# A two-layer hybrid decoder step: FFN up projections as seven products of halves, the gated product kept in DRAM, the down projection in three groups

## The chip, the cores and the metric

The kernel runs on one core of one Trainium2 chip. The core has a matrix engine (TensorE, PE in the profile, with its weight loads as PEld), a vector engine (VectorE, DVE), an activation engine (ScalarE, ACT), GpSimd (POOL), and a queue engine (SyncE, SP) from which this kernel issues all its DMAs. SBUF is the on-chip memory of 128 partitions; PSUM is where TensorE writes, and this kernel has five PSUM banks for its main products and three for side work. The metric is the device time of one execution in microseconds.

## The reference

One inference step of a two-layer decoder for 1024 prompt positions and 8 x 8 sample positions, 1088 columns in all, model width 1024. Layer 0 mixes with a convolution module and a retention in parallel, layer 1 with a gated linear recurrence. Each mixer is followed by the same gated convolution FFN, and this is where the change lies:

```python
def _conv_ffn(h, buf, w_up, conv_w, conv_b, w_down):
    z = h @ w_up
    zc, new_buf = _causal_dwconv(z, buf, conv_w, conv_b)
    g, u = jnp.split(zc, 2, axis=-1)
    return (jax.nn.gelu(g) * u) @ w_down, new_buf
```

Here `h` is the RMS-normalised residual (1088 x 1024), `w_up` is 1024 x 5632 (2816 gate and 2816 value columns), the convolution runs over positions with width 3, and `w_down` is 2816 x 1024. The result is added to the residual. The last two rows of `z` of each sequence are an output too. All arithmetic is float32.

## The kernel before

Everything is kept feature-major: 128 features on the partitions, positions as columns. `X` (8 feature tiles of 1088 columns) is the residual. A matrix product in float32 is made of three TensorE matmuls: each operand is split into a rounded high part and a low part that is the rest, and `mm3` (line 157) adds high x high, high x low and low x high in one PSUM bank. `HH` and `HL` hold the two parts of the normalised residual. Every `matmul` call comes with its own weight load. Columns are cut into blocks `TT` of 384, 384 and 320.

Weights come as 188 tiles of 128 x 1024 in a fixed order. `load_to` (line 111) fetches one into a raw buffer, lets ACT write the high part (line 118) and DVE the low part (line 119), and `get_w` (line 123) stays a stated number of tiles ahead.

The program text gives an order of emission. The framework that builds the kernel puts the instructions on each engine in that priority, and takes a later one first if the earlier one isn't ready by its own reckoning; each engine then works its queue strictly in order. Work that rides along (norms, retention, gates) is written as generators in the list `side`; after every sixth main matmul one step of the first generator is emitted (`mm`, `tick`, lines 151 and 135). `flush` emits what is left.

`rmsnorm` (line 183) does one column block: squares on ACT and sums on DVE, a transpose and a reduction, the root, a transpose back, then for each of eight feature tiles a scaling on DVE (line 224) and a split (lines 179 and 180). The output projections (`out_proj`, line 242, and the end of `even_mixer`) do their last feature tiles block by block, so that the norm of one block rides along under the next block's matmuls.

`ffn` (line 266) walks over 22 pairs, each a gate tile and a value tile of 128 features. `pair` (line 276) makes the two up products, 8 k tiles x 3 matmuls for each of the three column blocks, and ACT copies them from PSUM to `Z` rows. `act` (line 302) does the convolution with three DVE instructions a tile (lines 307 to 309), the GELU on ACT (line 314), the gated product on DVE (line 316), and its split into `A` (lines 319 to 323). POOL copies the edges of `Z` (lines 284, 311 and 312). `down` (line 327) follows two pairs behind: it multiplies the `A` of two pairs with their down weights and adds each 128 x 384 result to `X` (`add_x`, line 176). The last four pairs go together, block by block, with the next norm behind each block.

Of the kernel before, what the change touches and what calls it, by code (L numbers as in the profile page):

```python
# [26 lines left out]
# column offsets in the packed parameter tile  # L27
# [12 lines left out]
# columns of the shape-only constants of the retention  # L40
# [40 lines left out]
def hybrid_step(ctx: ExitStack, tc: tile.TileContext, I, O):  # L81
# [5 lines left out]
    wpool = ctx.enter_context(tc.tile_pool(name="wpool", bufs=5))  # L87
    rawp = ctx.enter_context(tc.tile_pool(name="rawp", bufs=2))
    tmpp = ctx.enter_context(tc.tile_pool(name="tmpp", bufs=5))
# [10 lines left out]
    HH = big.tile([P, KD, NT], F32R, name="HH")  # L100
    HL = big.tile([P, KD, NT], F32R, name="HL")
# [5 lines left out]
    # ---------------------------------------------------------------- weights  # L107
    state = {"loaded": 0, "next": 0}
    wtiles = {}

    def load_to(n):
        while state["loaded"] < min(n, len(ORDER)):
            i = state["loaded"]
            raw = rawp.tile([P, 1024], F32, tag="raw", name="raw")
            nc.sync.dma_start(raw, I["w"][i])
            ws = wpool.tile([P, 2, KD, P], F32R, tag="ws", name="ws")
            whi = ws[:, 0].rearrange("p k f -> p (k f)")
            nc.scalar.activation(whi, raw, AF.Copy)  # L118
            nc.vector.tensor_tensor(ws[:, 1].rearrange("p k f -> p (k f)"), raw, whi.bitcast(F32), ALU.subtract)  # L119
            wtiles[i] = ws  # L120
            state["loaded"] += 1
# [8 lines left out]
    # Work that rides along: generators whose steps are emitted between the  # L130
    # matmuls of the main stream, one step to about a microsecond of them.
# [9 lines left out]

    def flush(gen=None):
        """Emits what is left of the generators up to gen, or of all."""
# [7 lines left out]
    def mm(out, lhsT, rhs, start, stop):  # L151
        nc.tensor.matmul(out, lhsT, rhs, start=start, stop=stop)  # L152
        count[0] += 1
        if count[0] % TICK == 0:
            tick()

    def mm3(out, w_hi, w_lo, x_hi, x_lo, start, stop):
        mm(out, w_hi, x_hi, start, False)
        mm(out, w_hi, x_lo, False, False)
        mm(out, w_lo, x_hi, False, stop)  # L160

    def mm_group(ws, t):
        """Weight tiles over one column block, the contraction outermost."""
        t0, n = TT[t]
        pss = [mmp.tile([P, 512], F32, tag="mm", name="mm") for _ in ws]
        for k in range(KD):
            for w, ps in zip(ws, pss):
                mm3(ps[:, :n], w[:, 0, k], w[:, 1, k], HH[:, k, t0:t0 + n], HL[:, k, t0:t0 + n], k == 0, k == KD - 1)
        return pss

# [11 lines left out]
    # ------------------------------------------------- 1/sqrt of column sums  # L182
    def rmsnorm(t, g, final=False, spill_after=False):
        """RMSNorm of one column block of X into HH and HL, or into the output (a generator)."""
        t0, n = TT[t]
        acc = tmpp.tile([P, 512], F32, tag="tmp", name="acc")
        for m in range(KD):
            if m == 0:
                nc.scalar.activation(acc[:, :n], X[:, m, t0:t0 + n], AF.Square)
            else:  # L190
                sq = tmpp.tile([P, 512], F32, tag="tmp", name="sq")
# [24 lines left out]
        for m in range(KD):  # L216
# [6 lines left out]
            hn = tmpp.tile([P, 512], F32, tag="tmp", name="hn")  # L223
# [5 lines left out]
    # residual to DRAM and back, one column block at a time  # L229
# [11 lines left out]
    # ------------------------------------------------------ output projection  # L241
    def out_proj(key, norm_g):
        NE = 3
        for m in range(NE):
            w = get_w((key, m))
            for t in range(3):
                add_x(m, t, mm_tile(w, t))
        ws = [get_w((key, m), ahead=KD - 1 - m) for m in range(NE, KD)]
        for t in range(3):
# [757 lines left out]
```

## Time and profile before

| | |
|---|---|
| median of 3 runs | 2389.2 us (2389.01 to 2390.93) |
| profiled execution: span | 2388.6 us |
| profiled execution: its own time | not listed apart; the median lies 0.6 us above the span |
| PE busy | 2362.4 us, 99%, 14368 matmuls |
| PEld busy | 2332.5 us, 98% |
| DVE busy | 1463.3 us, 61% |
| ACT busy | 811.9 us, 34% |
| POOL busy | 154.7 us, 6% |
| mean granted TensorE clock | 0.996 |
| DMA | 133.28 MB, mean 56 GB/s |

The page gives the busy time of each engine, the chain of work that ended last (each step followed back to what released it), and the costliest groups of instructions: line, engine, operation, output and input tiles, count, then busy time and mean duration of one, then the idle time of the engine ahead of them and what ended it. A window row has the busy time and instruction count of each engine in a stretch, the granted clock as a share of full, the share of the DMA engines and GB/s. A timeline row has the start in us, the duration, the engine, the line and the instruction. Matmul records overlap, so their busy time isn't the sum of their durations.

### The profile page before, as it was taken

To read this page: it belongs to the slowest core of one execution; us is meant where nothing else is said; L and a number is where in the kernel's file an instruction comes from. 1 tells how busy PE (TensorE), PEld (TensorE's weight loads), DVE (VectorE), ACT (ScalarE), POOL (GpSimd) and SP (SyncE) were. 2 spreads that over 40 slices of the span, in tenths; PEclk is the share of its full clock that TensorE was granted. 3 is DMA by queue.
4 is the path that set the end of the run, shared out by engine and by line. 5 is a ranking of instruction groups with operands and counts; after the bars stand their busy time and mean duration, and the time that the engine had idled before them with its cause. 6 is when DMAs were issued, how large, how long until landed. Compare 5 with 4: busy or idle time off the path is not lost.

```text
span 2388.6 us, 34372 instructions
## 1 busy us (share of the span) xinstructions
PE 2362.4 (99%) x14368; PEld 2332.5 (98%) x14368; DVE 1463.3 (61%) x2209; ACT 811.9 (34%) x1500; POOL 154.7 (6%) x409
## 2 busy tenths in 40 slices
PE   9999999999999999999999999999999999999998
PEld 8999999999999999999999999999999999999997
DVE  6899965575554455555467757476455555455546
ACT  6334437342222222222235667243222222222222
POOL 0000000010000000000000211001000000000000
PEclk9999999999999999999999999999999999999999
DMA  5212114111111111111113111411111111111102
GB/s 181 67 46 64 55 37 115 39 62 44 45 36 54 45 45 45 45 36 54 45 60 131 36 36 36 119 45 54 45 45 45 45 36 54 45 45 45 45 29 80
DMA packets 64509, 133.28 MB, mean 56 GB/s; under 512 B 24097, under 2 KB 37281, under 8 KB 64225
## 3 DMA queue, kind: packets, MB, share of 16 engines
q1 hardware_dynamic: 64352, 131.08, 17.4%
q8 instruction: 113, 1.85, 0.3%
q14 instruction: 44, 0.35, 0.1%
HBM read 118.28 MB, written 12.78 MB: 55 GB/s over the span
## 4 chain that ended last, share of the span: by engine, by line
PE 93%; DVE 3%; ACT 2%; DMA 1%; issue 1%; DVEq 0%; SPq 0%; ACTq 0%
PE mm L152 89%; DVE acc L193 1%; PE ax L852 0%; PE ax L545 0%; PE ax L536 0%; DMA X<-in_x 0%; DVE ws L119 0%; PE ax L527 0%; PE ax L507 0%; PE ax L495 0%; PE ax L759 0%; DVE X L774 0%; PE ax L479 0%; PE ax L529 0%; PE ax L760 0%
## 5 line engine op out<-in xcount | busy, mean ns | idle before, releaser
L152 PE MATMUL mm<-HH,ws 128*128 128x384 f32 (+1 forms) x6912 | 1715.5, 328 | 0.6 <-ACT HH L854 0.5
L152 PEld LDWEIGHTS mm<-HH,ws 128*128 128x128 f32 x6912 | 1223.3, 188 | 8.9 <-issue 6.8
L152 PE MATMUL mm<-HL,ws 128*128 128x384 f32 (+1 forms) x3456 | 1129.2, 327 | 4.1 <-DVE HL L180 4.1
L152 PEld LDWEIGHTS mm<-HL,ws 128*128 128x128 f32 x3456 | 650.0, 188 | 5.1 <-DVE HL L180 4.7
L152 PE MATMUL mm<-A,ws 128*128 128x384 f32 (+1 forms) x3168 | 528.0, 328 | 0.4 <-ACT A L319 0.4
L152 PEld LDWEIGHTS mm<-A,ws 128*128 128x128 f32 x3168 | 522.5, 188 | 1.3 <-ACT A L319 1.0
L119 DVE TENSOR_TENSOR ws<-raw,ws 128x1024 fp32r<-128x1024 f32 x188 | 228.0, 1222 | 306.7 <-ACT ws L118 306.5
L176 DVE TENSOR_TENSOR X<-X,mm 128x384 f32<-128x384 f32 (+1 forms) x540 | 277.2, 530 | 157.2 <-PE mm L152 148.4
L118 ACT ACTIVATE ws<-raw 128x1024 fp32r<-128x1024 f32 x188 | 197.1, 1059 | 395.9 <-PE mm L152 390.6
L307 DVE TENSOR_SCALAR Y<-Z,par 128x1104 f32<-128x1104 f32 x88 | 74.8, 852 | 273.7 <-ACT Z L299 273.7
L295 ACT ACTIVATE Z<-mm 128x384 f32<-128x384 f32 x176 | 86.7, 493 | 360.1 <-PE mm L152 360.0
L413 DVE SCALAR_TENSOR_TENSOR X<-U,par,X 128x1024 f32<-128x1024 f32 x120 | 151.7, 1280 | 0.0
L311 POOL COPY fst<-Z 128x2 f32<-128x2 f32 x88 | 52.2, 593 | 1181.6 <-ACT Z L298 1181.6
L319 ACT ACTIVATE A<-Y 128x1024 fp32r<-128x1024 f32 x44 | 46.7, 1062 | 222.0 <-DVE Y L316 222.0
L308 DVE SCALAR_TENSOR_TENSOR Y<-Z,par,Y 128x1104 f32<-128x1104 f32 x88 | 120.2, 1367 | 2.3
L309 DVE SCALAR_TENSOR_TENSOR Y<-Z,par,Y 128x1104 f32<-128x1104 f32 x88 | 120.1, 1366 | 1.5
L298 ACT ACTIVATE Z<-mm 128x256 f32<-128x256 f32 x88 | 33.0, 375 | 126.9 <-PE mm L152 126.9
L322 DVE TENSOR_TENSOR A<-Y,A 128x1024 fp32r<-128x1024 f32 x44 | 53.8, 1223 | 29.3 <-ACT A L319 29.3
L314 ACT ACTIVATE Y<-Y 128x1104 f32<-128x1104 f32 x44 | 49.6, 1128 | 54.7 <-DVE Y L309 54.7
L192 ACT ACTIVATE sq<-X 128x384 f32<-128x384 f32 (+1 forms) x84 | 39.8, 502 | 77.4 <-DVE X L176 69.8
L316 DVE TENSOR_TENSOR Y<-Y 128x1104 f32<-128x1104 f32 x44 | 57.4, 1305 | 0.8
L193 DVE TENSOR_TENSOR acc<-acc,sq 128x384 f32<-128x384 f32 (+1 forms) x84 | 44.9, 534 | 16.3 <-ACT sq L192 12.1
(193 smaller groups left out, 1229.9 us busy)
## 6 DMA issues: line engine op xcount, KB each, us to landing
raw<-in_w SPq DMA_DIRECT2D x188, 512.0 KB, 3.5
X<-in_xt SPq DMA_DIRECT2D x8, 512.0 KB, 7.9
X<-in_x SPq DMA_DIRECT2D x4, 768.0 KB, 5.3
spill<-X SPq DMA_DIRECT2D x2, 1536.0 KB, 5.8
X<-spill SPq DMA_DIRECT2D x2, 1536.0 KB, 10.3
out_y<-X SPq DMA_DIRECT2D x4, 768.0 KB, 3.4
S<-in_st_ret SPq DMA_DIRECT2D x4, 512.0 KB, 3.5
out_s_ret<-S SPq DMA_DIRECT2D x4, 512.0 KB, 2.6
```

The source lines that it names most:

```text
L118: nc.scalar.activation(whi, raw, AF.Copy)
L119: nc.vector.tensor_tensor(ws[:, 1].rearrange("p k f -> p (k f)"), raw, whi.bitcast(F32), ALU.subtract)
L152: nc.tensor.matmul(out, lhsT, rhs, start=start, stop=stop)
L176: nc.vector.tensor_tensor(X[:, m, t0:t0 + n], X[:, m, t0:t0 + n], ps[:, :n], ALU.add)
L193: nc.vector.tensor_tensor(acc[:, :n], acc[:, :n], sq[:, :n], ALU.add)
L295: nc.scalar.activation(z[:, 2 + t0:2 + t0 + n], ps[:, :n], AF.Copy)
L307: nc.vector.tensor_scalar(y, z[:, 2:NE], pc(fw, 2 * 44 + f), pc(fb, f), ALU.mult, ALU.add)
L308: nc.vector.scalar_tensor_tensor(y, z[:, 1:NE - 1], pc(fw, 44 + f), y, ALU.mult, ALU.add)
L309: nc.vector.scalar_tensor_tensor(y, z[:, 0:NE - 2], pc(fw, f), y, ALU.mult, ALU.add)
L316: nc.vector.tensor_tensor(Y[0], Y[0], Y[1], ALU.mult)
L322: nc.vector.tensor_tensor(a[:, 1, :NP], y[:, :NP], a[:, 0, :NP].bitcast(F32), ALU.subtract)
L413: nc.vector.scalar_tensor_tensor(cv, U[i][:, j:j + NP], wj, cv, ALU.mult, ALU.add)
```

## The change

The up projection of one pair is a product of a 1024 x 256 weight (two k halves x gate and value tile) with 1024 x 1088 activations (two k halves x two column halves of 544). After, it is made by a scheme of seven products of halves (Winograd's form of Strassen's algorithm) in place of the eight: each product has 4 k tiles and 272 columns, twice, for the two blocks `SB` of each half. Sums of operands are made before the products and sums of results after:

- `norm_halves` takes the place of `rmsnorm` ahead of an FFN. It works on blocks `TB` (208, 208 and 128 columns of each column half), stores the residual to DRAM (`spill`), scales `X` in place, and writes seven split operands: four into `HB` (the old `HH` and `HL`), three into a new tile `HX`.
- `Pair` loads the two raw weight tiles of a pair and makes seven split weight operands of 128 x 512, with four combinations on DVE, the high parts on ACT and the low parts on POOL. The next pair's are made while a pair's products run, two steps in its first half block and the rest in its second.
- `block` runs the seven products of one half block in four PSUM banks (three of them are accumulated into again after they were read) and adds up the results into `Z`.
- `X` is free during the up products and holds `Z`, `Y` and the other rows of the FFN.
- `act` starts the convolution on ACT in place of DVE (Identity with scale and bias); the gated product isn't split, but stored to DRAM (`yd`).
- The down projection comes after all 22 pairs, in three groups of 8, 6 and 8 feature tiles. `fetch` loads a stored product and splits it, into `HB` for the first and third group and `A2` for the second. The first group's result is added to the stored residual, which makes `X` again; the others are added to `X`.
- The last four feature tiles of an output projection run in the blocks `TB` (`proj_tail`), weight tiles are split in two halves (`wpool` of 10 half tiles in place of 5 whole), and the general temporaries are 4 of 544 columns in place of 5 of 512.

```diff
+NH = NT // 2
+TB = [(0, 208), (208, 208), (416, 128)]
+SB = [(0, 272), (272, 272)]
+GROUPS = (8, 6, 8)
...
     for p in range(NFF):
         o += [("up%d" % l, p), ("up%d" % l, NFF + p)]
-        if p % 2 == 0 and 2 <= p <= NFF - 4:
-            o += [("dn%d" % l, p - 2), ("dn%d" % l, p - 1)]
-    o += [("dn%d" % l, q) for q in range(NFF - 4, NFF)]
+    o += [("dn%d" % l, (g, m)) for g in range(len(GROUPS)) for m in range(KD)]
...
+    class Pair:
+        def steps(self):
+            r1, r2 = self.raws
+            a11, a12, a21, a22 = r1[:, :512], r1[:, 512:], r2[:, :512], r2[:, 512:]
+            def put(src):
+                w, hi, lo = split_w(src)
+                nc.gpsimd.tensor_tensor(lo, src, hi.bitcast(F32), ALU.subtract)
+                self.w.append(w)
+            v = nc.vector
+            s3 = self.pool.tile([P, 512], F32, tag="s3", name="s3", bufs=1)
+            v.tensor_tensor(s3, a11, a21, ALU.subtract)
+            put(a11)
+            yield
+            v.tensor_tensor(a21, a21, a22, ALU.add)
+            put(s3)
+            yield
+            put(a21)
+            yield
+            v.tensor_tensor(a11, a21, a11, ALU.subtract)
+            put(a11)
+            yield
+            put(a12)
+            yield
+            v.tensor_tensor(a12, a12, a11, ALU.subtract)
+            put(a22)
+            yield
+            put(a12)
...
+    def norm_halves(b, g, spill, HX):
+        o, n = TB[b]
+        N = 2 * n
+        nc.sync.dma_start(spill, halves(X, o, n))
...
+        for kk in (0, 2):
+            for k in (kk, kk + 1, kk + 4, kk + 5):
+                xm = halves(X[:, k], o, n)
+                nc.vector.scalar_tensor_tensor(xm, xm, pc(g, k), rb, ALU.mult, ALU.mult)
...
+            def put(src, k, c):
+                hi, lo = (HB[(slice(None), e) + part(k, c)] if c < 2 else HX[:, e, c - 2, kk:kk + 2, o:o + n]
+                          for e in (0, 1))
+                nc.scalar.activation(hi, src, AF.Copy)
+                nc.vector.tensor_tensor(lo, src, hi.bitcast(F32), ALU.subtract)
...
+            put(b11, kk, 0)
+            t3 = diff(b22, b12)
+            put(t3, None, 3)
+            t1 = diff(b12, b11)
+            put(t1, kk, 1)
+            t2 = diff(b22, t1)
+            put(t2, None, 2)
+            put(b21, kk + 4, 0)
+            t4 = diff(b21, t2)
+            put(t4, None, 4)
+            put(b22, kk + 4, 1)
+            yield
...
+    def proj_tail(m0, ws, ffn):
+        ffn.start()
+        for b in range(3):
+            o, n = TB[b]
+            for m, w in enumerate(ws):
+                ps = mm_halves(w, HACTS, b)
+                xm = halves(X[:, m0 + m], o, n)
+                nc.vector.tensor_tensor(xm, xm, ps, ALU.add)
+                if b == 2:
+                    ffn.first.make(2)
+            side.append(ffn.norm(b))
...
+            MOVE = (0, 5, 1, 4, 2, 6, 3)
+            def product(w, i, sb, ps, first):
+                o, n = SB[sb]
+                for k in range(4):
+                    mm3(ps[:, :n], w[:, 0, k], w[:, 1, k], moving(MOVE[i], 0, k, o, n), moving(MOVE[i], 1, k, o, n),
+                        first and k == 0, k == 3, more=not first)
...
+                p1 = bank()
+                product(W.w[0], 0, sb, p1, True)
+                nc.scalar.activation(u2[:, :n], p1[:, :n], AF.Copy)
+                after(0)
+                p7 = bank()
+                product(W.w[1], 1, sb, p7, True)
+                after(1)
+                p5 = bank()
+                product(W.w[2], 2, sb, p5, True)
+                after(2)
+                p6 = bank()
+                product(W.w[3], 3, sb, p6, True)
+                v.tensor_tensor(u2[:, :n], u2[:, :n], p6[:, :n], ALU.add)
+                v.tensor_tensor(u3[:, :n], u2[:, :n], p7[:, :n], ALU.add)
+                high(z2, u3, p5)
+                after(3)
+                product(W.w[4], 4, sb, p1, False)
+                nc.scalar.activation(low(z1), p1[:, :n], AF.Copy)
+                after(4)
+                product(W.w[5], 5, sb, p7, False)
+                v.tensor_tensor(low(z2), u2[:, :n], p7[:, :n], ALU.add)
+                after(5)
+                product(W.w[6], 6, sb, p5, False)
+                high(z1, u2, p5)
+                after(6)
...
+                    nc.scalar.activation(y, z[:, 2:NE], AF.Identity, bias=pc(fb, f), scale=pc(fw, 2 * 44 + f))
+                    v.scalar_tensor_tensor(y, z[:, 1:NE - 1], pc(fw, 44 + f), y, ALU.mult, ALU.add)
+                    v.scalar_tensor_tensor(y, z[:, 0:NE - 2], pc(fw, f), y, ALU.mult, ALU.add)
...
+                nc.sync.dma_start(self.yd[p], YG)
...
+            def fetch(f, sb, hi, lo):
+                o, n = SB[sb]
+                t = tmpp.tile([P, 544], F32, tag="tmp", name="yl")
+                tv = t.rearrange("p (h c) -> p h c", h=2)
+                nc.sync.dma_start(tv, halves(self.yd[f], o, n))
+                nc.scalar.activation(halves(hi, o, n), tv, AF.Copy)
+                v.tensor_tensor(halves(lo, o, n), tv, halves(hi, o, n).bitcast(F32), ALU.subtract)
+            W = self.first
+            W.make(8)
+            flush_all_but_last()
+            for p in range(NFF):
+                if p:
+                    prepare(p)
+                nxt = self.pair(p + 1) if p + 1 < NFF else None
+                def after_a(i):
+                    if nxt and i in (3, 6):
+                        nxt.make()
+                def after_b(i):
+                    if nxt:
+                        nxt.make()
+                    else:
+                        fetch(i, 0, *HACTS[i])
+                block(p, W, 0, after_a)
+                if p:
+                    act(p - 1)
+                flush()
+                if not p:
+                    prepare(p)
+                block(p, W, 1, after_b)
+                if nxt:
+                    nxt.make(8)
+                W = nxt
+            fetch(7, 0, *HACTS[7])
+            load_to(state["next"] + 3)
+            for q in range(8):
+                fetch(q, 1, *HACTS[q])
+            act(NFF - 1)
...
+                def first_block(w, m, b):
+                    o, n = TB[b]
+                    t = tmpp.tile([P, 544], F32, tag="tmp", name="xr")
+                    tv = t[:, :2 * n].rearrange("p (h c) -> p h c", h=2)
+                    nc.sync.dma_start(tv, self.spill[b][:, m])
+                    ps = mm_halves(w, HACTS, b)
+                    v.tensor_tensor(halves(X[:, m], o, n), tv, ps, ALU.add)
...
+                for m in range(4):
+                    w = get_w((key, (2, m)), ahead=3)
+                    for t in range(3):
+                        add_x(m, t, down(w, HACTS, t))
+                ws = [get_w((key, (2, m)), ahead=KD - 1 - m) for m in range(4, KD)]
+                for t in range(3):
+                    for m in range(4, KD):
+                        add_x(m, t, down(ws[m - 4], HACTS, t))
+                    side.append(rmsnorm(t, norm_next, final, spill_after=not final))
```

More of the change, by code (lines that the diff above doesn't have):

```diff
@@ L140, in tick, with flush_all_but_last @@
                 side.popleft()
+    def flush_all_but_last():
+        while len(side) > 1:
+            for _ in side.popleft():
+                pass
     def flush(gen=None):
@@ L149, in flush, with mm @@
                 break
-    def mm(out, lhsT, rhs, start, stop):
-        nc.tensor.matmul(out, lhsT, rhs, start=start, stop=stop)
+    def mm(out, lhsT, rhs, start, stop, more=False):
+        nc.tensor.matmul(out, lhsT, rhs, start=start, stop=stop, skip_group_check=more)
         count[0] += 1
@@ L155, in mm, with mm3 @@
             tick()
[L157 to L160, printed above, removed]
+    def mm3(out, w_hi, w_lo, x_hi, x_lo, start, stop, more=False):
+        mm(out, w_hi, x_hi, start, False, more)
+        mm(out, w_hi, x_lo, False, False, more)
+        mm(out, w_lo, x_hi, False, stop, more)
     def mm_group(ws, t):
@@ L185, in rmsnorm @@
         t0, n = TT[t]
[L186 removed]
+        acc = tmpp.tile([P, 544], F32, tag="tmp", name="acc")
         for m in range(KD):
@@ L325, in act @@
-                return a
-            def down(p0, acts, last):
-                nq = len(acts)
-                wd = [get_w((dn, p0 + q), ahead=4) for q in range(nq)]
-                order = [(t, m) for t in range(3) for m in range(KD)] if last else \
-                        [(t, m) for m in range(KD) for t in range(3)]
-                for t, m in order:
+                        nc.scalar.activation(YG[:, :NP], y[:, :NP], AF.Gelu_apprx_tanh)
+                        nc.scalar.activation(YG[:, NP:].rearrange("p (b s) -> p b s", s=8), sample_view(y, 1026, 10),
+                                             AF.Gelu_apprx_tanh)
@@ new lines, in down @@
+                    return ps
+                for m in range(KD):
+                    w = get_w((key, (1, m)), ahead=3)
+                    for t in range(3):
+                        add_x(m, t, down(w, A2, t))
+                        if todo:
+                            fetch(*todo.pop(0))
+                while todo:
+                    fetch(*todo.pop(0))
+                for m in range(4):
+                    w = get_w((key, (2, m)), ahead=3)
+                    for t in range(3):
+                        add_x(m, t, down(w, HACTS, t))
@@ L657, in even_mixer @@
                     half_mm(ws[q - 2], 0, q, t)
-        ws = [get_w(("oab", m)) for m in range(4)]
-        for t in range(3):
-            for m in range(4):
-                add_x(m, t, mm_tile(ws[m], t))
-            side.append(rmsnorm(t, "nffn0"))
+        ws = [get_w(("oab", m), ahead=3 - m) for m in range(4)]
+        f = FFN(0)
+        proj_tail(0, ws, f)
+        return f
     def odd_mixer():
```

319 lines of the change are left out of this document (208 added, 111 removed).

## Prediction

> **What bounds the kernel now.** Read first: the page's busy times and its chain by line; then the two FFN bodies as windows (PE, PEld, DVE, ACT and POOL busy, granted clock, DMA share, GB/s); then single matmuls in the timeline.
>
> ```profile
> span 2388.6 us, 34372 instructions
> PE 2362.4 (99%) x14368; PEld 2332.5 (98%) x14368; DVE 1463.3 (61%) x2209; ACT 811.9 (34%) x1500; POOL 154.7 (6%) x409
> ...
> PE mm L152 89%; DVE acc L193 1%; PE ax L852 0%; PE ax L545 0%; PE ax L536 0%; DMA X<-in_x 0%; DVE ws L119 0%; PE ax L527 0%; PE ax L507 0%; PE ax L495 0%; PE ax L759 0%; DVE X L774 0%; PE ax L479 0%; PE ax L529 0%; PE ax L760 0%
> ```
>
> ```profile
> 493.00:1219.00 726.00, 726.00 (x4412) 725.96 (x4412) 389.51 (x486) 178.47 (x309) 55.45 (x170) 1.00 0.14 45
> 1600.00:2328.00 728.00, 728.00 (x4426) 728.00 (x4424) 388.17 (x483) 177.85 (x309) 55.20 (x170) 1.00 0.13 43
> ```
>
> The matmuls of line 152 are 89% of the chain. In the FFN bodies (61% of the span) they leave no hole, the clock is full, DVE is at 54%. So only the number and size of matmuls counts there, and any hole that the change opens is paid in full. A record lasts longer than its share of the array, so the price of a matmul is the distance between like records. First two of 384 columns, then two of 320, each three matmuls apart:
>
> ```profile
> 804.45 0.33 PE L152 MATMUL mm<-HL,ws 128*128 128x384 f32 x1
> ...
> 804.97 0.33 PE L152 MATMUL mm<-HL,ws 128*128 128x384 f32 x1
> ...
> 801.08 0.31 PE L152 MATMUL mm<-HL,ws 128*128 128x320 f32 x1
> ...
> 801.52 0.31 PE L152 MATMUL mm<-HL,ws 128*128 128x320 f32 x1
> ```
>
> 0.52/3 = 173.3 ns and 0.44/3 = 146.7 ns: 0.4167 ns a column and 13.3 ns a matmul. By that line 272 columns cost 126.7, 416 cost 186.7, 256 cost 120 ns.
>
> **The change, term 1: the products.** An up pair (gate tile and value tile) has 2 x 8 x 3 = 48 matmuls in each of three column blocks; after, 7 products x 4 x 3 = 84 in each of two blocks of 272. Per layer: 22 x 48 x (173.3 + 173.3 + 146.7) ns = 520.9 us before, 22 x 168 x 126.7 ns = 468.3 us after: 52.6 us less, 105.2 in two layers. The smaller matmul must not be held by its weight load. The weight loads below belong to 128-column matmuls with full 128x128 weights; two take 0.22 us, 110 ns each, and 126.7 lies above that.
>
> ```profile
> 129.00 0.30 PEld L527 LDWEIGHTS ax<-vtm,scm 128*128 128x128 f32 x2
> 129.22 0.30 PEld L529 LDWEIGHTS ax<-S,X 128*128 128x128 f32 x2
> ```
>
> The down projection keeps its 22 x 8 x 3 x 3 = 1584 matmuls per layer, and 416 + 416 + 256 columns cost as much as 384 + 384 + 320. So its first group and the output projection's tail in halves are even. Its adds into X fall from 240 to 72 a layer, on an engine that isn't the bound: nothing. Weight splitting in half tiles, four temporaries for five, and a lookahead of 3 for 4 cost nothing while PE is fed by five PSUM banks; uncovered, a lost load costs the 3.5 us to landing below, a few times.
>
> **Term 2: the start of each FFN.** The norm now makes seven split operands of each half product. For each block and each k pair it is 4 scalings, 7 subtractions and 4 differences on DVE, so 30 DVE operations a block where there were 16 (and the 7 sums of squares in both). Durations by form (busy, mean ns, idle before), and how they run one behind another:
>
> ```profile
> L176 DVE TENSOR_TENSOR X<-X,mm 128x384 f32<-128x384 f32 x360 | 193.3, 552 | 112.4 <-PE mm L152 104.7 <-DMA X<-spill 4.6 <-DMA X<-in_x 2.9
> L176 DVE TENSOR_TENSOR X<-X,mm 128x320 f32<-128x320 f32 x180 | 87.0, 487 | 44.7 <-PE mm L152 43.7 <-DMA X<-spill 0.2
> L224 DVE SCALAR_TENSOR_TENSOR hn<-X,par,ax 128x384 f32<-128x384 f32 x48 | 27.0, 610 | 4.5 <-PE ax L213 4.5
> L119 DVE TENSOR_TENSOR ws<-raw,ws 128x1024 fp32r<-128x1024 f32 x188 | 228.0, 1222 | 306.7 <-ACT ws L118 306.5
> ```
>
> ```profile
> 1558.70 1.49 DVE L180 TENSOR_TENSOR HL<-hn,HH 128x384 fp32r<-128x384 f32 x3
> ...
> 1571.71 0.55 DVE L176 TENSOR_TENSOR X<-X,mm 128x384 f32<-128x384 f32 x1 [1.15 <-PE mm L152]
> ...
> 1577.78 1.66 DVE L224 SCALAR_TENSOR_TENSOR hn<-X,par,ax 128x384 f32<-128x384 f32 x3
> ...
> 1585.61 0.56 DVE L180 TENSOR_TENSOR HL<-hn,HH 128x384 fp32r<-128x384 f32 x1 [0.16 <-ACT HH L179]
> 1586.08 1.28 DVE L176 TENSOR_TENSOR X<-X,mm 128x320 f32<-128x320 f32 x3
> ```
>
> About 1 ns a column: 0.44 us for 272, 0.69 for 512; run together 0.50 instead of 0.55 at 384, so some 0.54 at 416 and 0.39 at 256. From the last add of a block to its first scaling is 6.1 us (1571.71 to 1577.78). And the adds of the next block wait behind the whole norm: three of them come in one batch after its last subtraction (1586.08). Let 0 be the end of the tail's first block of matmuls. PE runs block two (96 x 186.7 ns) to 17.9 and block three (96 x 120) to 29.4. DVE: norm one from 6 to 6 + 30 x 0.54 = 22.3, 24 with adds between; then block two's last add and 6.1 us, so norm two scales from 30.5. The first product needs 20 of its 30 operations (both k pairs' scalings, the first pair whole, one split): 41.3. PE has waited 12 us. Norm three follows norm two's end (46.7) with its squares and chain, some 5 us, and is needed after 20 x 0.39 us: 59.5, while the first half block ends at 41.3 + 84 x 0.1267 = 52: another 7.5. The first pair's weights come from POOL in the same stretch and hold DVE off for part of it; I add 5: 25 us a layer, 50 in all. Bounds a layer: 12, if the second wait fills, and 35, if norm three and the half block's own adds queue behind each other. Copying X out before it is scaled in place stays inside the 6 us:
>
> ```profile
> raw<-in_w SPq DMA_DIRECT2D x188, 512.0 KB, 3.5
> ...
> spill<-X SPq DMA_DIRECT2D x2, 1536.0 KB, 5.8
> ```
>
> An idle array also loses its clock for a while; early in the kernel, after such holes, the granted clock (third number from the end) is 0.79 over 8 us:
>
> ```profile
> 12.00:20.00 8.00, 7.38 (x38) 6.58 (x39) 6.67 (x12) 7.38 (x18) 0.00 (x0) 0.79 0.84 312
> ```
>
> 8 x 0.21 = 1.7 us; once a layer 3.4 in all.
>
> **Term 3: the steady pairs.** A pair now takes PE 168 x 126.7 ns = 21.3 us. Its DVE work: ten PSUM adds of 272 columns (one extra split twice), 4.7 us; four weight combinations, 2.75; four multiply-adds and the gated product, 6.9; together 14.4. ACT has about 9.5. Both fit. What matters is order:
>
> ```profile
> L308 DVE SCALAR_TENSOR_TENSOR Y<-Z,par,Y 128x1104 f32<-128x1104 f32 x88 | 120.2, 1367 | 2.3
> L316 DVE TENSOR_TENSOR Y<-Y 128x1104 f32<-128x1104 f32 x44 | 57.4, 1305 | 0.8
> L314 ACT ACTIVATE Y<-Y 128x1104 f32<-128x1104 f32 x44 | 49.6, 1128 | 54.7 <-DVE Y L309 54.7
> L118 ACT ACTIVATE ws<-raw 128x1024 fp32r<-128x1024 f32 x188 | 197.1, 1059 | 395.9 <-PE mm L152 390.6
> ```
>
> The sixth product accumulates into the bank that u3 reads, so it waits for two adds (2 x 0.44) after the fourth product, while the fifth (12 x 126.7 ns = 1.52 us) runs. With 0.25 for the handover, 0.39 us is left. A multiply-add of 1.37 us that is under way then delays it by 0 to 1.37, over the slack by 0.98 squared / 2 / 1.37 = 0.35 us on average. The first half block of a pair, where the previous pair's gate is worked, has DVE nearly full; the second hasn't. So 0.35 a pair, 15.4 us for 44. Bounds: 0, and 88 (2 us a pair) if something else sits ahead of the multiply-add.
>
> That something is POOL, which splits the seven weight operands (512 columns, two inputs), an operation the trace doesn't have. Its nearest row writes 512 columns with no input. The other rows show a 16-column copy that takes 0.2 us elsewhere waiting 3.53 us, to the end of DVE's chain:
>
> ```profile
> L370 POOL MEMSET Qm<- 128x512 f32 x1 | 0.5, 524 | 0.3 <-POOLq L971 0.3
> ```
>
> ```profile
> 513.88 3.53 POOL L284 COPY Z<-fst 128x16 f32<-128x16 f32 x1
> ...
> 514.92 1.21 DVE L119 TENSOR_TENSOR ws<-raw,ws 128x1024 fp32r<-128x1024 f32 x1
> 516.06 1.30 DVE L316 TENSOR_TENSOR Y<-Y 128x1104 f32<-128x1104 f32 x1
> ```
>
> So the price is at least 0.52 us and, with three passes, 1.57; I take two passes, 1.05, 7.3 us a pair. POOL and DVE exclude each other while both read SBUF. DVE's operations of that kind are 9.7 us a pair, the rest read PSUM; 9.7 + 7.3 and six small copies (1.2) is 18.2 of 21.3, so POOL keeps up, and the products of a pair's weights have a half block of lead.
>
> The Trainium skill says the same more strictly (SBUF — State Buffer, Who interferes with whom): a DVE instruction with two SBUF inputs and a GpSimd instruction that reads SBUF take the shared port pair as an exclusive lock, the second waiting for the first to finish. The 3.53 us copy agrees for one direction; no row shows DVE held by POOL. The skill's GPSIMD Engine Reference (Performance versus the Vector engine) has 4497 ns for an fp32 add of 2048, so an estimate of 1.12 us for 512; by it the sum would not move, but the margin shrinks by 0.5 us a pair.
>
> **Term 4: up to down, and DRAM.** Eight fetches (0.72 us of DVE each) fit under the last half block, 10.6 us. The other eight and the last gate, 12.7 us of DVE, lie under three 416-column groups, 13.4 us: nearly full, 3 us a layer, 0 to 8. The stored product, the copy of X and their return are about 67 MB in all against 133 in the span; the DMA share of 0.14 covers them. On SP's queue the store of a product stands behind weight loads of the pair after, of which two buffers are always ahead.
>
> **Sum.** 2388.6 - 105.2 + 50 + 3.4 + 15.4 + 6 = 2358.2; the time is 0.6 above the span (2389.2 to 2388.6), so **2359 us**.
>
> **Rivals.** (a) The covers hold: only PE's first wait is paid, 12 us a layer, with clock, and no steady stall: 2388.6 - 105.2 + 24 + 3.4 + 0.6 = 2311. For it: ready work is pulled forward and PE had no holes. Against: 60 us of DVE in a tail of 29. (b) DVE and POOL take turns: if POOL's splits run only when DVE stands still, a pair takes 14.4 + 7.3 + 1.2 = 22.9 us against 21.3, 1.6 x 44 = 70 us instead of 15: 2413, slower. It decides from (21.3 - 14.4 - 1.2)/7 = 0.81 us a split, if nothing of POOL runs under DVE's PSUM adds; at 1.57 it would be 2576. For it the waiting copies; against it 4.7 us of PSUM adds and the idle third of DVE. (It is the lock of the Trainium skill, SBUF — State Buffer, Who interferes with whom, taken to its end.) (c) Small matmuls don't get cheaper: at 146.7 ns the up products take 542 us a layer, 21.3 more than now: 2388.6 + 42.6 + 74.8 + 0.6 = 2507; the 110 ns loads speak against it. (d) The stalls come to the 105 saved: 2389.
>
> **How the numbers follow.** Forecast 0.47, with its own range 2330 to 2383; (a) 0.25; (b) 0.18; (c) 0.02; (d) 0.08. Range 2303 to 2420. No change means within 0.2%, what a measurement of this kernel can tell. Faster 0.72, same 0.08, slower 0.20.
>
> **What would show it.** Products of 272 columns 126.7 ns apart, windows of 21.3 us a pair in the body; a hole of about 12 us in PE before the first product of each FFN and a second half as long, both released by DVE's subtractions; POOL rows near 1.05 us. Wrong would be: body pairs well above 21.7 us, PE waiting there for POOL's splits or DVE; no hole at the start; distances that don't fall with the columns.

## The result, and the profile after

The changed kernel takes 2564.5 us (median of four runs, 2559.5 to 2571.1), the kernel before on the same chip 2390.1. The ratio is 1.0728, with a 95% interval of 1.071 to 1.0746: 174 us slower, where 2359 us was forecast, and outside the range of 2303 to 2420.

The page of the changed kernel: the span, busy time by engine, the two lines of slices that matter, the chain by engine and line, then groups (count, busy time and mean ns of one, idle time before them with its releaser) and the weight loads with their time to landing.

```profile
span 2562.0 us, 38303 instructions
...
PE 2358.4 (92%) x15428; PEld 2311.5 (90%) x15428; DVE 1564.9 (61%) x2637; ACT 987.1 (39%) x1818; POOL 627.8 (25%) x637
...
PE   9999999888888888899999999978888888899998
...
PEclk9999999898888888999999999989998998899999
...
PE 17%; DVE 5%; DMA 4%; issue 3%; POOL 2%; ACT 1%; DVEq 0%; ACTq 0%
...
L222 PE MATMUL mm<-HX,ws 128*128 128x272 f32 x3168 | 497.6, 310 | 155.3 <-DVE X L534 150.3
...
L167 POOL TENSOR_TENSOR ws<-raw,ws 128x512 fp32r<-128x512 f32 x264 | 390.5, 1486 | 770.1 <-ACT ws L119 766.4
...
L552 DVE SCALAR_TENSOR_TENSOR X<-X,par 128x1104 f32<-128x1104 f32 x88 | 156.9, 1818 | 0.0
...
L551 DVE SCALAR_TENSOR_TENSOR X<-X,par 128x1104 f32<-128x1104 f32 x88 | 143.3, 1630 | 0.1
...
L172 DVE TENSOR_TENSOR s<-raw 128x512 f32<-128x512 f32 x44 | 35.8, 815 | 68.3 <-DMA raw<-in_w 68.2
...
raw<-in_w SPq DMA_DIRECT2D x176, 512.0 KB, 3.7
```

Line 222 is now the matmul (152 before), 551 and 552 are the multiply-adds (308 and 309 before), 167 the split of a weight operand on POOL, 172 the first combination of raw weights on DVE, 533 and 534 the adds that make `u2` and `u3`. No engine but PE is above 61%, and PE has lost its 99%: the two stretches of eights in its slices are the two FFN bodies. The chain, which was 89% matmuls, now accounts for a third of the span in pieces, so it doesn't name the bound. One wait does: the first matmul of the sixth product waits 150.3 us in all for `u3` (line 534). The multiply-adds, 1367 ns each before, take 1630 and 1818 ns with the same shapes.

The waits by engine, line and releaser, with total, count and longest:

```profile
PE mm L222 <- DVE X L534: 150.3, 43, 5.0
DVE raw L185 <- POOL ws L167: 147.7, 41, 3.9
...
DVE s L172 <- DMA raw<-in_w: 68.2, 40, 3.1
```

43 of the 44 pairs have that hole, 3.5 us on average. How long a pair lasts is read from the store of its product (queue of SP; the last column but one gives the first and the last of a layer's 22):

```profile
L563 SPq DMA_DIRECT2D yd<-X x22: 319/327/332, 546.4 to 1107.5; - x22
```

(1107.5 - 546.4)/21 = 26.7 us a pair, where 21.3 + 0.35 was forecast. In the same way the second layer has 26.8. Windows of both bodies, then of one hole and of the time behind it (PE, PEld, DVE, ACT, POOL busy with counts, granted clock, DMA share, GB/s):

```profile
600.00:1000.00 400.00, 347.45 (x2490) 344.16 (x2488) 224.14 (x321) 136.13 (x222) 198.39 (x193) 0.89 0.18 61
1640.00:2040.00 400.00, 342.39 (x2389) 335.22 (x2388) 252.36 (x395) 148.06 (x259) 181.95 (x174) 0.91 0.20 66
808.50:813.20 4.70, 0.00 (x0) 0.00 (x1) 4.70 (x6) 1.32 (x3) 2.37 (x3) 0.73 0.00 0
813.20:817.00 3.80, 3.80 (x17) 3.80 (x18) 2.00 (x4) 0.17 (x2) 0.00 (x0) 0.50 0.37 149
```

Over the first body DVE is busy 56% of the time, in the hole 100%. Behind the hole the clock is 0.50 for 3.8 us. One pair's hole in the timeline (start, duration; idle time and releaser in brackets):

```profile
800.06 0.21 DVE L518 TENSOR_TENSOR X<-X,mm 128x64 f32<-128x64 f32 x1
800.34 2.50 ACT L550 ACTIVATE X<-X,par 128x1104 f32<-128x1104 f32 x2
...
801.08 1.66 PE L222 MATMUL mm<-HX,ws 128*128 128x272 f32 x12
...
803.33 0.69 DVE L172 TENSOR_TENSOR s<-raw 128x512 f32<-128x512 f32 x1 [3.05 <-DMA raw<-in_w]
803.94 1.36 DVE L551 SCALAR_TENSOR_TENSOR X<-X,par 128x1104 f32<-128x1104 f32 x1
804.10 1.67 PE L222 MATMUL mm<-HX,ws 128*128 128x272 f32 x12
...
804.83 1.62 POOL L167 TENSOR_TENSOR ws<-s,ws 128x512 fp32r<-128x512 f32 x1 [2.75 <-ACT ws L119]
805.22 1.78 DVE L175 TENSOR_TENSOR raw<-raw 128x512 f32<-128x512 f32 x1
805.60 2.67 PE L222 MATMUL mm<-HB,ws 128*128 128x272 f32 x20
806.93 1.35 DVE L551 SCALAR_TENSOR_TENSOR X<-X,par 128x1104 f32<-128x1104 f32 x1
...
807.75 1.66 POOL L167 TENSOR_TENSOR ws<-raw,ws 128x512 fp32r<-128x512 f32 x1 [1.29 <-ACT ws L119]
808.21 3.64 DVE L552 SCALAR_TENSOR_TENSOR X<-X,par 128x1104 f32<-128x1104 f32 x2
...
811.77 0.42 DVE L533 TENSOR_TENSOR X<-X,mm 128x272 f32<-128x272 f32 x1
...
812.12 0.68 DVE L180 TENSOR_TENSOR raw<-raw 128x512 f32<-128x512 f32 x1
812.72 0.42 DVE L534 TENSOR_TENSOR X<-X,mm 128x272 f32<-128x272 f32 x1
...
813.20 1.05 PE L222 MATMUL mm<-HX,ws 128*128 128x272 f32 x3 [4.92 <-DVE X L534]
```

DVE works its queue in order. At its head stands line 172, a combination of the next pair's weights, and waits 3.05 us for a load that has not landed; behind it stand the multiply-adds, of which the first could have begun at about 801.6, when ACT's first of two scalings was done. Then two DVE instructions run beside a split on POOL: line 175 takes 1.78 us where its like in line 180 takes 0.68, and ends when POOL's does (804.83 + 1.62 = 806.45, and 0.55 more); the two of line 552 take 3.64 together. `u2` is made at 811.77, one more combination stands ahead of `u3`, and when that comes PE has stood still for 4.92 us. In this hole the lengthened instructions make 2.0 us (1.78 - 0.68, and 3.64 - 2 x 1.36), and the wait for the load 1.7 (803.33 - 801.6).

The load is late because its buffer is: there are two raw buffers, and the pair's last splits on POOL read them. They run in the second half block, and the next loads are issued behind them:

```profile
822.70 2.94 POOL L167 TENSOR_TENSOR ws<-raw,ws 128x512 fp32r<-128x512 f32 x2 [0.19 <-ACT ws L119]
824.42 1.58 SPq L124 DMA_DIRECT2D raw<-in_w  x2
```

The first of those two splits ends at about 824.2, the second at 825.6; the two loads are issued at 824.42 and about 825.7, and land 3.7 us later. 825.7 + 3.7 is 829.4; line 172's start at 803.33 has its counterpart one pair on, at 830.16, again behind a wait for the load.

So two readings were open when the experiments began. LOCK: POOL's splits, which read SBUF, hold up DVE's instructions with two SBUF inputs. LATE: the raw weights come late because POOL frees their buffers late, and stand at the head of DVE's queue.

### The profile page after: what moved, and what is told of

It reads as the page before. It is cut to its first block, busy times and chain, and to the rows that moved or that the text cites. A ratio compares the mean times of both kernels' runs of the same rounds, so it can differ in the third digit from the quotient of the medians.

```text
span 2562.0 us, 38303 instructions
## 1 busy us (share of the span) xinstructions
PE 2358.4 (92%) x15428; PEld 2311.5 (90%) x15428; DVE 1564.9 (61%) x2637; ACT 987.1 (39%) x1818; POOL 627.8 (25%) x637
## 5 line engine op out<-in xcount | busy, mean ns | idle before, releaser
L222 PE MATMUL mm<-HB,ws 128*128 128x272 f32 (+4 forms) x10560 | 1715.8, 319 | 18.7 <-ACT HB L368 9.1
L222 PEld LDWEIGHTS mm<-HB,ws 128*128 128x128 f32 x10560 | 1641.6, 195 | 34.1 <-ACT HB L368 11.1
L222 PE MATMUL mm<-HX,ws 128*128 128x272 f32 x3168 | 497.6, 310 | 155.3 <-DVE X L534 150.3
L222 PEld LDWEIGHTS mm<-HX,ws 128*128 128x128 f32 x3168 | 458.5, 207 | 167.3 <-DVE X L534 160.3
L167 POOL TENSOR_TENSOR ws<-raw,ws 128x512 fp32r<-128x512 f32 x264 | 390.5, 1486 | 770.1 <-ACT ws L119 766.4
L119 ACT ACTIVATE ws<-raw 128x512 fp32r<-128x512 f32 x472 | 290.4, 622 | 737.3 <-PE mm L222 536.3
L263 DVE TENSOR_TENSOR X<-X,mm 128x384 f32<-128x384 f32 (+1 forms) x132 | 69.8, 529 | 153.0 <-PE mm L222 143.9
L552 DVE SCALAR_TENSOR_TENSOR X<-X,par 128x1104 f32<-128x1104 f32 x88 | 156.9, 1818 | 0.0
L551 DVE SCALAR_TENSOR_TENSOR X<-X,par 128x1104 f32<-128x1104 f32 x88 | 143.3, 1630 | 0.1
L222 PE MATMUL mm<-A,ws 128*128 128x384 f32 (+1 forms) x864 | 142.7, 327 | 0.0
L222 PEld LDWEIGHTS mm<-A,ws 128*128 128x128 f32 x864 | 142.4, 188 | 0.0
L172 DVE TENSOR_TENSOR s<-raw 128x512 f32<-128x512 f32 x44 | 35.8, 815 | 68.3 <-DMA raw<-in_w 68.2
```

What stands on the lines that cost most here:

```text
L119: nc.scalar.activation(hi, src, AF.Copy)
L167: nc.gpsimd.tensor_tensor(lo, src, hi.bitcast(F32), ALU.subtract)
L172: v.tensor_tensor(s3, a11, a21, ALU.subtract)
L222: nc.tensor.matmul(out, lhsT, rhs, start=start, stop=stop, skip_group_check=more)
L263: nc.vector.tensor_tensor(X[:, m, t0:t0 + n], X[:, m, t0:t0 + n], ps[:, :n], ALU.add)
L551: v.scalar_tensor_tensor(y, z[:, 1:NE - 1], pc(fw, 44 + f), y, ALU.mult, ALU.add)
```

## The experiments

Periods are worked out from the stores as above, for the first layer; "hole" is PE's wait for `u3`. The kernel before took 2389.0 to 2391.0 us beside these runs, and each ratio is against it.

**e1_memset.** POOL writes zeros in place of the low parts of the up weights: it reads nothing and holds no raw buffer.

```
-                nc.gpsimd.tensor_tensor(lo, src, hi.bitcast(F32), ALU.subtract)
+                nc.gpsimd.memset(lo.bitcast(F32), 0.0)
```

> Leaves out the low parts of the up weights: POOL writes zeros (512 columns, nothing read) in place of its subtraction, so POOL keeps its place in the order but never takes a read port. Theory LOCK (POOL's subtractions hold DVE, whose multiply-adds take 1630 and 1818 ns here against 1367 before, some 2 us of the 3.4 us hole a pair): multiply-adds back at 1367 ns, hole near 1.4 us, too short for the clock to fall, time near 2390 us. Theory LATE (the next pair's raw weights arrive late and stand at the head of DVE's queue): multiply-adds shorter, but the hole stays above 2 us and the time above 2500 us.

2376.1 us, 0.9938 (0.9924 to 0.9953): 188 us off the changed kernel by one line. The multiply-adds are back at 1362 and 1360 ns, and the period is 22.5 us. The hole is left at a third:

```profile
PE mm L222 <- DVE X L534: 47.8, 40, 2.2
```

It is POOL, then. But this takes several things away at once: the reads, the hold on the raw buffers, and more than half of POOL's time; and the framework put DVE's instructions in another order.

**e2_lo_dve.** The same subtractions on DVE, so that all work is there and POOL reads no weights.

```
-                nc.gpsimd.tensor_tensor(lo, src, hi.bitcast(F32), ALU.subtract)
+                nc.vector.tensor_tensor(lo, src, hi.bitcast(F32), ALU.subtract)
```

> The seven low parts of a pair's weights are made on DVE in place of POOL, nothing else changed: no lock, but 7 x 0.69 = 4.8 us more DVE work a pair, 19.2 of 21.3. LOCK: about 2 us less waiting, of which the new subtractions that fall ahead of the adds eat a part: 2440 to 2520 us. LATE: the hole stays or grows by the new subtractions in front of the adds: 2560 to 2640 us.

2355.5 us, 0.985 (0.9834 to 0.9867): better than either reading allowed. Seven subtractions of 0.69 us load DVE with 4.8 us more a pair, to 319 of 400 us in the body, yet the period falls to 21.85 and the hole to 30.4 us in all. I had priced those 4.8 us as a delay of `u3`; most of them went into time in which DVE was idle.

**e3_raw4.** POOL keeps its splits; four raw buffers instead of two. To make room there are nine split buffers instead of ten.

```
-    wpool = ctx.enter_context(tc.tile_pool(name="wpool", bufs=10))
-    rawp = ctx.enter_context(tc.tile_pool(name="rawp", bufs=2))
+    wpool = ctx.enter_context(tc.tile_pool(name="wpool", bufs=9))
+    rawp = ctx.enter_context(tc.tile_pool(name="rawp", bufs=4))
```

> Raw weight buffers 4 in place of 2 (and 9 half weight tiles in place of 10, for room): the next pair's two raw tiles can be loaded a whole pair ahead. LATE: DVE no longer stands 1.7 to 3.3 us for the load, the hole falls to about 1 us, the clock stays full, time near 2390 us. LOCK: the hole stays at 2 us or more, time above 2480 us.

2466.3 us, 1.0313 (1.0298 to 1.0329), between the two. With loads in time 98 of the 174 us are gone, so LATE is a part; the kernel is still slower than before, and the hole now comes in both half blocks:

```profile
PE mm L222 <- DVE X L534: 106.1, 82, 2.3
```

```profile
L185 DVE TENSOR_TENSOR raw<-raw 128x512 f32<-128x512 f32 x44 | 32.5, 739 | 223.9 <-POOL ws L167 223.9
```

The multiply-adds take 1361 and 1381 ns here, so they are hardly held any more. In the second half block `u3` is late for another reason: line 185, a combination that stands ahead of it in DVE's queue, overwrites weights that POOL still has to read, and waits for that. At 798.12 it starts after 5.54 us of such waiting, and 0.67 us of PE's hole lie behind it. In the first half block line 172 waits for POOL in the same way, 43.7 us in all. So POOL delays DVE in two ways, by holding up an instruction that runs and by keeping one waiting for its read. The order on DVE changed too (line 172 now stands behind a multiply-add), so the 98 us are not the load's alone.

**e4_fill.** To price the clock by itself: 24 matmuls of 272 columns, whose result nobody reads, ahead of the sixth product in the first half block of each pair but the first of a layer.

```
+                if sb == 0 and p:
+                    fill = axp.tile([P, 512], F32, tag="ax", name="ax")
+                    for _ in range(24):
+                        nc.tensor.matmul(fill[:, :n], W.w[4][:, 0, 0], moving(0, 0, 0, o, n), start=True, stop=True)
                 product(W.w[5], 5, sb, p7, False)
```

> Adds 24 matmuls of 272 columns that nobody reads (24 x 126.7 ns = 3.04 us) to each first half block after the first pair, between the fifth and sixth product, where the hole is. Theory CLOCK (a hole of over 3 us halves the granted clock for the next 4 us, some 1.9 us a pair beside the hole): although PE gets 42 x 3.04 = 128 us more work, the time falls to 2470 to 2510 us and the granted clock in the body goes back to 1.00. If the hole alone were the loss: 2550 to 2580 us.

2545.4 us, 1.0645 (1.0629 to 1.0661): PE has 24 x 42 x 0.1254 = 126 us more to do, and the kernel is 19 us faster. The clock over the first body went from 0.89 to 1.00 (in the second layer's window from 0.91 to 0.95):

```profile
600.00:1000.00 400.00, 379.75 (x2998) 376.43 (x2997) 236.34 (x341) 144.66 (x236) 197.96 (x205) 1.00 0.19 65
```

So the clock behind the hole is a cost of its own. The expected 2470 to 2510 was missed, though: 64.1 us of waiting is left, and filling plus waiting (3.0 + 1.5 us a pair) is longer than the hole was. I put that down to DVE and POOL, whose chain sets the hole's end whatever PE does meanwhile; that is argued, not tried.

**e5_dve_raw4, e11_dve_raw3.** Both cures together: subtractions on DVE, and four raw buffers with nine split buffers (e5), or three with ten kept (e11).

```
-    rawp = ctx.enter_context(tc.tile_pool(name="rawp", bufs=2))
+    rawp = ctx.enter_context(tc.tile_pool(name="rawp", bufs=3))
...
-                nc.gpsimd.tensor_tensor(lo, src, hi.bitcast(F32), ALU.subtract)
+                nc.vector.tensor_tensor(lo, src, hi.bitcast(F32), ALU.subtract)
```

> Low parts on DVE and four raw buffers (nine half weight tiles). With no lock left, LATE is what remains: if the late load is the rest of the hole (0.7 us a pair with low parts on DVE alone), the hole goes to about 0.2 us and the time to 2330 to 2345 us. If the rest comes from DVE's own order (19.2 us of work in 21.3), nothing moves: 2350 to 2365 us.

> Low parts on DVE and three raw buffers, with the ten half weight tiles kept: the buffer count alone against e2. If the late load made e2's remaining hole: between 2324 (four buffers) and 2356 us, near 2335. If it was the order that four buffers and nine tiles brought: 2350 to 2360 us.

e5: 2323.9 us, 0.9719 (0.9704 to 0.9733). e11: 2317.2 us, 0.9695 (0.968 to 0.9709). Both are a little below what was expected. A window of e11's body shows PE without a hole, at full clock:

```profile
600.00:1000.00 400.00, 400.00 (x3100) 398.17 (x3099) 324.92 (x537) 174.01 (x287) 54.03 (x104) 1.00 0.30 95
```

With e2 and e3 these make a square: 2564 (POOL, two raw), 2466 (POOL, four), 2356 (DVE, two), 2324 (DVE, four). Read as it stands, a late load costs 98 us with POOL's splits beside it and 32 without them; POOL's splits cost 209 us with late loads and 142 with early ones. Neither alone makes the whole loss, and each makes the other worse. The square isn't clean, since the runs with four buffers have one split buffer less and another order on DVE; e5 and e11, which differ in these, lie 7 us apart. The cleanest step for the load is the one from e2 to e11, one raw buffer more: 38 us, and line 172's wait for it falls from 29.6 us in all to 2.2.

**e6_dve_bank5, e7_dve_both, e12_best.** The hole is a wait for `u3` because the sixth product accumulates into the bank that `u3` reads. Here it has its own bank, and the sum is made when it is read: e6 is that with e2, e7 that with e5, e12 that with e11.

```
-                product(W.w[5], 5, sb, p7, False)
-                v.tensor_tensor(low(z2), u2[:, :n], p7[:, :n], ALU.add)
+                p4 = bank()
+                product(W.w[5], 5, sb, p4, True)
+                v.tensor_tensor(low(z2), u3[:, :n], p4[:, :n], ALU.add)
```

> Low parts on DVE, and the sixth product goes to a bank of its own (the fifth) in place of the one that u3 is still to read; its result is then u3 plus the new bank, the same number of adds. If the wait for u3 is all of the remaining hole, it goes away and the next wait (the seventh product for the add that reads its bank) is one product later: 2325 to 2340 us. If a late DVE only moves the hole to that next wait: 2345 to 2360 us.

> Both of the above. If they are separate causes: 2315 to 2335 us, the body at 21.3 us a pair and the rest at the start of each FFN. If they are one: as the better of the two.

> Low parts on DVE, three raw buffers, ten half tiles and the sixth product in a bank of its own. If three buffers do as well as four: 2310 to 2325 us, not far from e7's 2315. If both raw tiles must be ahead: 2330 to 2350 us.

e6: 2353.6 us, 0.9845 (0.983 to 0.986), as e2. The wait only moved, to the seventh product and the add that its bank waits for:

```profile
PE mm L222 <- DVE X L516: 30.3, 37, 1.8
```

DVE was late, and any bank it empties would be. e7: 2315.5 us, 0.9685 (0.9671 to 0.9699); e12: 2317.2, 0.9692 (0.9676 to 0.9708), the same as e11 without it. Once the loads are early the bank is worth nothing with ten split buffers, and 8 us with nine. e7's stores give the price of a pair without holes:

```profile
L564 SPq DMA_DIRECT2D yd<-X x22: 320/327/333, 540.2 to 982.6; - x22
```

442.4/21 = 21.07 us.

**e8_dve_two.** Only the first two of a pair's seven subtractions on DVE, those that fall beside the multiply-adds.

```
-                nc.gpsimd.tensor_tensor(lo, src, hi.bitcast(F32), ALU.subtract)
+                eng = nc.vector if len(self.w) < 2 else nc.gpsimd
+                eng.tensor_tensor(lo, src, hi.bitcast(F32), ALU.subtract)
```

> Only the first two of a pair's seven low parts go from POOL to DVE; they fall into the first half block, beside the multiply-adds. The other five stay on POOL. LOCK says that only the subtractions beside the multiply-adds matter: multiply-adds near 1367 ns, time within 30 us of the 2356 of all seven on DVE. LATE says that the five on POOL still free the raw buffers late: hole of 1.5 us or more a pair, time above 2400 us.

2461.3 us, 1.0291 (1.0274 to 1.0309). 103 us better than the changed kernel, 106 worse than e2. The time is what LATE gave, but not for its reason: the first combination waits only 16.8 us in all for its load, where it was 68.2. The third split runs beside the multiply-adds still (lines are one further down here):

```profile
812.32 1.36 DVE L552 SCALAR_TENSOR_TENSOR X<-X,par 128x1104 f32<-128x1104 f32 x1
812.54 2.28 POOL L168 TENSOR_TENSOR ws<-raw,ws 128x512 fp32r<-128x512 f32 x1 [3.39 <-ACT ws L119]
...
813.60 2.39 DVE L553 SCALAR_TENSOR_TENSOR X<-X,par 128x1104 f32<-128x1104 f32 x1
...
818.02 0.65 PE L223 MATMUL mm<-HX,ws 128*128 128x272 f32 x3 [2.75 <-DVE X L535]
```

They take turns: the split starts under a multiply-add, which ends at 813.68, and takes 2.28 us for the 1.29 that it takes undisturbed (813.68 + 1.29 = 814.97; it ends at 814.82); the next multiply-add starts under the split and takes 2.39 for 1.36. This hole of 2.75 us is followed by a full clock, where the one of 4.92 us above was followed by 0.50:

```profile
818.00:822.00 4.00, 3.98 (x31) 3.98 (x32) 2.97 (x6) 0.99 (x3) 0.00 (x0) 1.00 0.19 71
```

The length of a hole alone doesn't decide it, though: behind another hole of this run, 2.73 us from 637.52 on, the clock was 0.50 over 4 us. Between the first and the last store of each layer, 10 of the 32 holes of 2 to 3 us in e8 were followed by a lowered clock, and 37 of the 38 holes over 3 us in the changed kernel.

**e9_memset_long, e10_act_first.** Is it POOL's reads, or only that a split takes 1.3 us? In e9 POOL writes 1280 columns of zeros per operand (1.32 us) and reads nothing. In e10 it has all its work; the multiply-adds of the previous pair are emitted ahead of the first half block.

```
-                nc.gpsimd.tensor_tensor(lo, src, hi.bitcast(F32), ALU.subtract)
+                [nc.gpsimd.memset(q.bitcast(F32), 0.0) for q in (lo, lo, lo[:, :256])]
```

```
+                if p:
+                    act(p - 1)
                 block(p, W, 0, after_a)
-                if p:
-                    act(p - 1)
```

> As e1 (low parts of the up weights left out), but POOL writes 1280 columns of zeros a split (512, 512 and 256): by 527 ns for 512 that is 1.32 us, as long as one of its subtractions when nothing disturbs it (1.29 us), and still without a read. DVE, ACT and PE have the order of e1 and e10. LOCK: DVE isn't held, multiply-adds 1367 ns, time within 25 us of e1's 2376. Theory LENGTH (what hurts is that weights, raw buffers and DVE's in-place combinations wait for a slow POOL): near e10, above 2480 us.

> The changed kernel with one thing moved: the previous pair's convolution and gate are emitted ahead of the first half block in place of behind it. All work is there. It has the DVE, ACT and PE order of e1 and e9, so against e9 it differs in POOL's two reads alone. LOCK: 2500 to 2570 us. If the order of emission (weight combinations ahead of the multiply-adds) had been the cause: under 2450 us.

e9: 2373.3 us, 0.9927 (0.9908 to 0.9946), as e1, though POOL is as busy (217 us of the body's 400) as in the changed kernel (198). Its multiply-adds:

```profile
L551 DVE SCALAR_TENSOR_TENSOR X<-X,par 128x1104 f32<-128x1104 f32 x88 | 116.8, 1363 | 1.0 <-ACT X L550 1.0
```

So long work on POOL costs nothing where it reads nothing. e10: 2495.2 us, 1.0442 (1.0415 to 1.0468), just under what LOCK gave. Against the changed kernel 69 us are gained by an order in which the multiply-adds don't stand behind a late load (line 172 waits 2.0 us in all for a DMA). The second multiply-add of a tile is held up as before:

```profile
L552 DVE SCALAR_TENSOR_TENSOR X<-X,par 128x1104 f32<-128x1104 f32 x88 | 157.8, 1829 | 0.0
```

The expectations took e1, e9 and e10 to have one order on DVE. In the traces e9 has that of e1, with lines 172 and 175 ahead of all four multiply-adds, and e10 has one of its own, with line 172 behind the first and line 175 behind the fourth. First e9, then e10:

```profile
660.90 0.69 DVE L172 TENSOR_TENSOR s<-raw 128x512 f32<-128x512 f32 x1 [1.83 <-DMA raw<-in_w]
...
662.53 2.64 DVE L551 SCALAR_TENSOR_TENSOR X<-X,par 128x1104 f32<-128x1104 f32 x2
```

```profile
659.10 1.37 DVE L551 SCALAR_TENSOR_TENSOR X<-X,par 128x1104 f32<-128x1104 f32 x1 [1.41 <-ACT X L550]
660.38 0.69 DVE L172 TENSOR_TENSOR s<-raw 128x512 f32<-128x512 f32 x1
```

So the comparison of e1 with e10 (119 us) is not one of POOL's reads alone, and e1's 188 us can't be split into an order and a rest. The order isn't what e1 and e9 gain by: in both, line 172 waits 82.0 us in all for its load, more than in the changed kernel, and the multiply-adds stand behind it. They gain by less time from line 172 to `u3` (8.1 us in the median, against 9.8), and by earlier loads: in one pair of e1 they are issued 13.3 us before the fifth product ends (788.62 and 801.92), in the pair shown above 12.0 (796.24 and 808.27). Writing zeros takes away both things that POOL's reads do, the hold on DVE's instructions and the wait for weights to have been read; how much each costs over the whole run was not taken apart.

## Why the prediction was wrong, by its steps

**Term 1, the products: right.** 21.07 us a pair are 21.07/168 = 125.4 ns a matmul where 126.7 was taken. The saving is 520.9 - 22 x 168 x 0.1254 = 57.4 us a layer, 115 in all for 105. Rival (c) is out.

**Term 2, the starts: right in size.** In the changed kernel the tail's last block, the first product of FFN 0 and the second half block begin so:

```profile
476.93 5.95 PE L222 MATMUL mm<-HB,ws 128*128 128x256 f32 x48 [1.89 <-DVE X L413]
...
490.56 0.59 PE L222 MATMUL mm<-HB,ws 128*128 128x272 f32 x1 [2.17 <-ACT HB L368]
...
514.54 2.17 PE L222 MATMUL mm<-HB,ws 128*128 128x272 f32 x6 [1.42 <-ACT HB L368]
```

From 482.9 (476.93 + 5.95) to 514.5 are 31.7 us for 84 products worth 10.5: 21 us, a part of it at a lowered clock. The second half block begins at a lowered clock too (0.50 from 514.5 to 520.5). 25 and 1.7 were forecast. The two waits are not the two single holes foreseen, since the first k pair's products are done while the second k pair is still being prepared.

**Term 4, up to down and DRAM: nothing.** PE is busy without a hole where a layer goes from up to down: 123.00 of the 123 us from 1107 on in the changed kernel, 125.00 of the 125 us from 985 on in e11. Without POOL's reads and with loads in time e11's span nearly comes out from terms 1 and 2 alone. Its starts are 18.5 and 18.1 us (483.42 to 512.48 and 1554.71 to 1583.38, less 10.5 each): 2388.6 - 115 + 36.6 = 2310, measured 2316.3. Its pairs, at 21.2 and 21.1 us, account for about half of the rest. So the 15.4 us of term 3 are not there either: this is rival (a) in the body, and its 2311 was near, by other terms.

**Term 3, the steady pairs: this step failed.** It took 0.35 us a pair. Measured are 26.7 - 21.07 = 5.6 us, of which the hole is 3.5 (150.3 us in 43 pairs) and the rest, 2.1, the clock behind it: 0.50 for 3.8 us is 1.9. Over the 42 pairs between first and last stores of two layers that is 5.6 x 42 = 235 us; 2388.6 - 115 + 42 + 235 = 2551, against a span of 2562.0. The 11 us that are left were not taken apart; the lowered clock of the second half blocks (6 us at 0.50 in the first layer, so 3) and shorter holes before a layer's first store (1.42 us up to 529.12, 2.04 up to 541.55) are among them. In the text three things went wrong:

- "so POOL keeps up": it was right as a sum (18.2 of 21.3 us), and beside the point. The sum asked whether POOL gets through its work, and looked at POOL waiting for DVE, the one direction that the trace showed. DVE waiting for POOL was never priced, and it falls on the one place of the pair with 0.39 us of slack. The split takes 1.29 us undisturbed against 1.05 taken; in e9 work of 1.32 us that reads nothing costs no more than e1's 0.53.
- "of which two buffers are always ahead", and "the products of a pair's weights have a half block of lead": the lead was counted up to the product, not up to the first combination, which stands in DVE's queue ahead of the multiply-adds. And it took the raw buffers to be free, while POOL's late splits hold them.
- The clock was charged at the two starts alone. A hole that comes 43 times, and is long enough, is charged 43 times.

The bound of 2 us a pair for "something else ahead of the multiply-add" was too low as well: it left out that what stands there may itself wait, and the clock.

**Rival (b)** named the engines, and its 2576 at 1.57 us a split is near the time. But not by its mechanism: it had the two engines taking turns all pair long, so that a pair is the sum of their work. They are not: e10 has all of POOL's splits and all of DVE's work, and takes 69 us less by order alone; e3 has them and takes 98 less by two more buffers and the order that came with them. What decides is the delay at one wait.

The Trainium skill (SBUF — State Buffer, Who interferes with whom) says that DVE and GpSimd share a port pair as an exclusive lock, that a DVE instruction with two SBUF inputs contends for it with a GpSimd instruction that reads SBUF and not with one that only writes, and that the order of issue decides who blocks. This case now agrees on all three: line 175 at 1.78 us for 0.68 beside a split, 1363 ns in e9, and e3, where a multiply-add that begins at 804.61 takes its 1.36 us and the split that begins at 804.77 takes 2.35. On the clock the skill (TensorE: Matmul & The Clock Gate, Part 1, What's actually happening) has half rate after an idle window of about 3.4 us, until as long a window has been busy. The 0.50 for 3.8 us behind a hole of 4.9 agrees; the lowered clock behind 10 of 32 holes of 2 to 3 us in e8 does not follow from it.

## What to carry to other kernels

When work is given to an idle engine, ask of both engines what each does to the other's instructions, and price it at the wait with the least slack, not as a share of busy time; moving these subtractions from an engine at 25% to one at 61% made the kernel 8% faster (e2 against the change). In an in-order queue look at what stands ahead of the urgent instruction and what that may wait for: here one more raw buffer (e11) took away the last of the holes and made the scheme 3.1% faster than the kernel before. On a kernel bound by TensorE, a hole of over 3 us that comes again and again costs its own length and, here, some 60% more in the clock; shorter ones sometimes do.

## What the runs showed that was not expected

- Unread matmuls paid: 126 us of them made the kernel 19 us faster, because the clock stayed higher, at 1.00 in the first layer's window for 0.89 (e4).
- A split of 512 columns on POOL takes 1.29 us undisturbed, 1.49 on average over 264, and 2.28 between two multiply-adds, the second of which goes from 1.36 to 2.39: both engines lose.
- DVE at 81% of the body (e11) leaves PE no hole, while at 56% with POOL beside it PE waits in 43 of 44 pairs: its busy share said nothing of how late it was.
